# Sums made ahead for the first feed-forward's first group alone, their loads behind VectorE, a ring of five raw tiles, and the memory stage's pools in another order

## The chip, the cores and the metric

The kernel runs on one core of one Trainium2 chip. The metric is device time in microseconds (us) of one execution, as the median of the runs; lower is better. Everything is float32 in DRAM.

## The reference, cut to what matters

One layer of a streaming encoder block works on 256 tokens of width 2048, with 256 memory tokens:

```python
x = x + 0.5 * swiglu(rms_norm(x, ffn1_norm), ffn1_w_up, ffn1_w_down)   # ffn1, hidden width 5632
h = rms_norm(x, mix_norm); proj = h @ w_in                             # the middle: two recurrences, gates
x = x + (sigmoid(gate_A) * y_A @ w_a + sigmoid(gate_B) * y_B @ w_b) @ w_out
x = x + cross_attention(rms_norm(x, xattn_norm), rms_norm(mem, mem_norm), wq, wkv, wo)
x = x + 0.5 * swiglu(rms_norm(x, ffn2_norm), ffn2_w_up, ffn2_w_down)   # ffn2, the same shape as ffn1
return rms_norm(x, final_norm)
def swiglu(h, w_up, w_down):
    gate, up = split(h @ w_up, 2); return (silu(gate) * up) @ w_down
```

Nearly all of the arithmetic is the product of the activations with weights that are each read once. The change touches how ffn1's and ffn2's up weights are prepared.

## The kernel before, in words

**Two parts per weight.** A weight tile is 128 x 2048 float32, 1 MiB, a "piece". TensorE multiplies a rounded format, so each piece is cut into a high part h, which ScalarE rounds (`split`, L147), and a low part l = raw - h, which VectorE subtracts (L148). Three products (h with the high activations `xh`, h with their low part `xl`, l with `xh`) stand for one exact one.

**Stages.** The memory stage computes values and keys of the memory tokens (32 pieces of `wvm` and `wk`; it ends at about 185 us). ffn1 follows to about 868 us, then the middle to about 1798 us, then ffn2. A feed-forward has 11 groups of hidden columns. A group has 8 up pieces, numbered 0 to 7, and from the second group on it is followed by some pieces of the down projection (`ffn_order`: two after groups 1 and 2, four later).

**Seven products for eight.** The up projection is done on 512-column blocks by a scheme that needs seven block products where eight would be usual, and needs sums of blocks. The sums of a piece are three VectorE instructions (L335, L337, L339) which write the tile `td`; `td` is then cut into a high and a low part (`tl`) like a weight. A string (`FIRST`, L46) gives each up piece of ffn1 a letter, in the order in which the pieces are used:

- `f`: load, three sums, l by VectorE.
- `a` ("added"): load, three sums, but l of the raw blocks without VectorE: ScalarE writes -h (L344), and a DMA issued by GpSimd reads the weight a second time and adds it on top (L345, 768 KB). ScalarE makes h after it (L346).
- `r` ("ready"): the sums have been made earlier and stored to DRAM as a tile `t`. Then the piece needs two loads: three of its blocks (768 KB, L318) and `td<-t` (1 MiB, L323), and no sum.

**Sums made ahead.** `make_ahead` (L205 to L215) makes one `t`: GpSimd issues the load of a `prep` tile (L208), VectorE makes four subtractions (L213), GpSimd issues the store (L214). `beside` (L219) starts one every few pieces: for ffn1's `r` pieces during the memory stage, for ffn2's during the middle. `with tc.issue_after(ins)` puts what follows behind `ins` only on the engine on which `ins` runs, so around L208 (GpSimd) with a VectorE instruction it orders nothing.

**Who waits for whom.** `weights` prepares pieces two ahead. Loads are issued by SP in one row, each when its tile is free; SP stands still while the next one is not. Raw tiles come from `rawp` (3 tiles) and, in ffn1, one more (`raw1`, every fourth, L272). `h` and `l` have 3 tiles each. In ffn1 `td` and `tl` come from a ring `wide` of 4, and a ready piece's `td` does too. In the memory stage other pools stand at the same addresses: `scope` gives pools memory in the order in which they are named, so the order decides which tile of ffn1 must wait for which tile of the memory stage. `mem` (6 tiles) holds operands of the memory products, which TensorE reads until the stage's last product; `prep`, `tmp`, `tmp2` and `norms` come free earlier. `three` (L600 to L606) issues a piece's products: L604 those with h, L606 those with l and `tl`. `ev` (L690 to L702) marks a group's end.

Of the kernel before, what the change touches and what calls it, by code (L numbers as in the profile page):

```python
# [8 lines left out]
F32 = mybir.dt.float32  # L9
# [4 lines left out]
P = 128  # L14
# [5 lines left out]
NG = DFF // 512  # L20
# [22 lines left out]


PIECES = "f1 a3 f0 a4 f2 a5 a6 f7"
FIRST = ["r1 r3 f0 a4 f2 a5 a6 f7"] + [PIECES.replace("f2", "r2") if g in (1, 2, 3) else PIECES for g in range(1, NG)]  # L46


def first(g):
# [23 lines left out]

def adds(name, e):

    return name == "ffn1" and e[0] == "fast" and f"a{e[2]}" in FIRST[e[1]]


def sums_ready(name, e):
# [8 lines left out]
def block_kernel(ctx: ExitStack, tc: tile.TileContext, xT, xin, memT, vec, gfin, bgate, lruw, wu1, wd1, win, wv,  # L88
                 wg, wab, wout, wq, wk, wvm, wo, wu2, wd2, out_):
    nc = tc.nc  # L90
    pe, dve, act, sp = nc.tensor, nc.vector, nc.scalar, nc.sync
# [65 lines left out]
    def plan_ffn(name, wu, wd):  # L157
        for e in orders[name]:
            src = wd[e[4], e[3]] if e[0] == "down" else wu[e[1], e[2]]
            kind = "fast" if e[0] == "fast" else "plain"  # L160
            if e[0] == "down" and 0 < e[4] < NG - 1 and e[4] % 2 == 0 and e[3] % 2:
                kind = "added"
            if adds(name, e):
                kind = "fast added"
            if kind == "fast" and (e[1] < 4 if name == "ffn2" else False):
                kind = "fast early"
            if sums_ready(name, e):
                kind = "ready"
                t = kept.tile([P, 2048], F32, name=f"t{e[1]}_{e[2]}")
                (made_first if name == "ffn1" else made_ahead).append((src, t))  # L170
                src = src, t
            plan.append(((name,) + e, src, kind))
# [29 lines left out]

    head, rest = [], {}

    def make_ahead(src, to):  # L205

        t = scoped["prep"].tile([P, 2048], F32, name="prep", tag="prep")
        nc.gpsimd.dma_start(t, src)  # L208
        yield
        b = [t[:, i * 512:(i + 1) * 512] for i in range(4)]  # L210
        with tc.issue_after(done["low"]):
            for o, x, y in ((1, 0, 1), (0, 0, 2), (2, 2, 1), (3, 3, 2)):
                dve.tensor_tensor(out=b[o], in0=b[x], in1=b[y], op=ALU.subtract)  # L213
        nc.gpsimd.dma_start(to, t)  # L214
        yield  # L215
# [3 lines left out]
    def beside(i):  # L219

        if under_way and (i >= under_way[0][0] or "prep" not in scoped):
            next(under_way.pop(0)[1])
        if "prep" not in scoped or i < turn[0]:
            return
        if i < first_ffn:
            if made_first:
                turn[0] = i + 5 if len(made_first) > 1 else first_middle + 2
                steps = make_ahead(*made_first.pop(0))
                with tc.issue_after(done["low"]):
                    next(steps)  # L230
                under_way.append((i + 3, steps))
        elif made_ahead and i < first_second - 4:
            early = "scores" in scoped
            turn[0] = i + (2 + len(made_ahead) % 2 if early else 3 if len(made_ahead) % 3 else 2)
            steps = make_ahead(*made_ahead.pop(0))
            next(steps)
            under_way.append((i + (2 if early or "kt" in scoped else 3), steps))
# [34 lines left out]
    def raw_tile():  # L272

        if "raw2" in scoped and next(loads) % 5 > 2:
            return scoped["raw2"].tile([P, 2048], F32, name="raw2", tag="raw2")
        if "raw1" in scoped and next(loads) % 4 == 3:
            return scoped["raw1"].tile([P, 2048], F32, name="raw1", tag="raw1")
        return rawp.tile([P, 2048], F32, name="raw", tag="raw")

# [9 lines left out]
    def prepare(src, kind, opens=None):  # L289

        if kind == "added":
            raw, l = begun.pop(0)
            h = hp.tile([P, 2048], F32R, name="h", tag="h")
            done["high"] = act.activation(h, raw, ACT.Copy).ins
            return h, l
        first = opens == 0
        raw = begun.pop(0) if first else raw_tile()
        n = 2048 if opens is None else 512
        if kind == "plain":
            h, l = split_tiles()  # L300
            for a in range(0, 2048, n):
                if a or not first:
                    sp.dma_start(raw[:, a:a + n], src if opens is None else in_blocks(src, n)[a // n * P:][:P])
                if first and a == n:
                    sp.dma_start(opening[1], block(528, 512))
                if first and not a:
                    dve.tensor_scalar(out=h[:, :n], in0=raw[:, :n], scalar1=1.0, scalar2=None, op0=ALU.mult)
                if opens is not None:
                    mem_operand(4 * opens + a // n)
                if first and not a:  # L310
                    done["low"] = dve.tensor_tensor(out=l[:, :n], in0=raw[:, :n], in1=h[:, :n].bitcast(F32),
                                                    op=ALU.subtract).ins
                else:
                    split(h[:, a:a + n], l[:, a:a + n], raw[:, a:a + n])
            return h, l
        if kind == "ready":
            src, t = src
            sp.dma_start(raw[:, 512:], src[:, 512:])  # L318
            if "raw2" not in scoped and "wide" in scoped:
                td = scoped["wide"].tile([P, 2048], F32, name="td", tag="wide")  # L320
            else:
                td = raw_tile()
            sp.dma_start(td, t)  # L323
        else:
            sp.dma_start(raw, src)
            early = kind == "fast early"
            if early:
                td = slot(name="td")
            elif "raw2" in scoped:
                td = raw_tile()  # L330
            else:
                td = scoped["wide"].tile([P, 2048], F32, name="td", tag="wide")
            third, fourth = (raw[:, :512], raw[:, 512:1024]) if early else (td[:, 1024:1536], td[:, 1536:])
            two = [v[:, a:a + 1024].rearrange("p (i n) -> p i n", i=2) for v, a in ((td, 0), (raw, 512))]
            dve.tensor_tensor(out=two[0], in0=raw[:, None, :512].broadcast_to([P, 2, 512]), in1=two[1],  # L335
                              op=ALU.subtract)
            dve.tensor_tensor(out=third, in0=raw[:, 1024:1536], in1=td[:, :512], op=ALU.subtract)  # L337
            if not early:
                dve.tensor_tensor(out=fourth, in0=raw[:, 1536:], in1=third, op=ALU.subtract)  # L339
        h, l = split_tiles()  # L340
        if kind != "fast added":
            split(h[:, 512:], l[:, 512:], raw[:, 512:])
        else:
            act.activation(l[:, 512:], raw[:, 512:], ACT.Copy, scale=-1.0)  # L344
            nc.gpsimd.dma_start(l[:, 512:], src[:, 512:], accum_op=ALU.add)  # L345
            done["high"] = act.activation(h[:, 512:], raw[:, 512:], ACT.Copy).ins  # L346
        halves = [td[:, a:a + 1024] for a in ((0,) if kind == "fast early" else (0, 1024))]
        if kind == "fast early":
            dve.tensor_tensor(out=fourth, in0=raw[:, 1536:], in1=third, op=ALU.subtract)
            halves.append(raw[:, :1024])  # L350
        th = hp.tile([P, 2048], F32R, name="h", tag="h")
        if "wide" in scoped:
            tl = scoped["wide"].tile([P, 2048], F32R, name="tl", tag="wide")
        else:
            tl = lp.tile([P, 2048], F32R, name="tl", tag="l")
        for a, t in zip((0, 1024), halves):
            split(th[:, a:a + 1024], tl[:, a:a + 1024], t)
        return (h, l), (th, tl)
# [123 lines left out]
            return r  # L482


    FFN1_POOLS = dict(wide=4, hd=1, raw1=1)
    FFN2_POOLS = dict(wide=2, raw2=2, hid=1, hd=1)

    class TokenSquares:
# [377 lines left out]
            split(s[:, :512], s[:, 512:], f)  # L866
            nc.gpsimd.dma_start(kept_v[2 * g + t], s)

    with scope(mem=6, tmp=6, tmp2=1, norms=1, prep=1):
        for g in range(4):  # L870
            values.append((g, [bank(), bank()]))
            for kq in range(4):
                rows_product(values[-1][1], ms.tiles, weights("mv", g, kq), 4 * kq, kq == 0, kq == 3, g == kq == 0)
            if g:
                keep_values()
        ks = Operands()
        for m in range(KT):
            ks.add(summed(product(ms.tiles, weights("k", m))[0]))
            if not m:
                keep_values()  # L880
            if m % 2:
                nc.gpsimd.dma_start(kept_k[m // 2], ks.cur)
# [590 lines left out]
```

## Time and profile before

| | |
|---|---|
| time, median of 3 runs (lowest to highest) | 2472.39 us (2471.56 to 2485.05) |
| the profiled execution | 2474.72 us, its span 2473.0 us |
| mean granted TensorE clock | 0.992 |
| busy: PE / VectorE (DVE) / ScalarE (ACT) / GpSimd (POOL) | 2408.2 / 2100.1 / 1510.1 / 131.7 us |
| DMA moved | 711.07 MB, 288 GB/s in the mean |

The span is the time from the first to the last instruction of the profiled execution; the 1.7 us beside it lie outside. A group row reads: line, engine, operation, output<-input by the program's names, shape, count, then busy time and mean ns, then the idle time before. A timeline row reads: start, duration, the same names, count, and in brackets the engine's idle time before and what ended it. A windows row reads: the stretch, its length, then busy time and count of PE, PEld, DVE, ACT and POOL, the granted TensorE clock, the DMA engines' share and GB/s. SPq and POOLq are issues of DMA.

### The profile page before, as it was taken

The numbers are of one execution on the slowest core, as the hardware profiler recorded it, in microseconds if no ns is written. First come the engines' busy times: TensorE is split into PE (matmuls) and PEld (weight loads), VectorE is DVE, ScalarE is ACT, GpSimd is POOL, SyncE is SP. The second block draws the span as 40 slices with busy tenths as digits, with TensorE's granted clock in tenths as the row PEclk, the third lists the DMA queues.
The fourth block names the chain that finished last, engine by engine and source line by source line (L and its number), as shares of the span: only waits on it lengthen the run. The fifth ranks groups of instructions, "written<-read, shape, count | busy, mean of one in ns | idle before, by whom it ended". The sixth has DMA issues, their size and how long they took to land.

```text
span 2473.0 us, 30918 instructions
## 1 busy us (share of the span) xinstructions
PE 2408.2 (97%) x12044; PEld 1997.1 (81%) x12044; DVE 2100.1 (85%) x2359; ACT 1510.1 (61%) x1551; POOL 131.7 (5%) x213
## 2 busy tenths in 40 slices
PE   9997888999999999999999999999999999999998
PEld 7885666888888888888888888888887788888887
DVE  7777888999999967778788877777799998999895
ACT  6655666777777754445457434554676666666663
POOL 0100000000000000000000000010000000000000
PEclk9998999999999999999999999999999999999999
DMA  8997778889999958887988998898687778787773
GB/s 314 351 343 239 221 228 244 271 272 276 275 277 276 276 196 332 303 317 286 347 310 285 384 342 335 313 358 305 255 322 264 279 273 288 271 290 274 285 274 150
DMA packets 109106, 711.07 MB, mean 288 GB/s; under 512 B 12128, under 2 KB 12640, under 8 KB 36256
## 3 DMA queue, kind: packets, MB, share of 16 engines
q1 hardware_dynamic: 78912, 519.56, 56.3%
q0 software_dynamic: 29904, 189.28, 25.7%
q8 instruction: 94, 1.54, 0.2%
q14 instruction: 52, 0.43, 0.0%
q10 hardware_dynamic: 144, 0.26, 0.0%
HBM read 637.62 MB, written 71.43 MB: 287 GB/s over the span
## 4 chain that ended last, share of the span: by engine, by line
PE 74%; DVE 4%; issue 3%; DMA 3%; ACT 2%; POOL 0%; ACTq 0%; POOLq 0%; DVEq 0%
PE acc L604 26%; PE acc L606 13%; PE acc L368 8%; PE acc L393 7%; PE acc L394 6%; PE acc L399 6%; PE acc L371 4%; DMA raw<-wu 2%; ACT h L147 1%; DVE l L148 1%; DMA l<-wu 1%; DVE tl L148 1%; PE acc L644 1%; PE acc L540 1%; PE acc L994 0%
## 5 line engine op out<-in xcount | busy, mean ns | idle before, releaser
L147 ACT ACTIVATE h<-raw 128x2048 fp32r<-128x2048 f32 (+3 forms) x558 | 834.9, 1522 | 602.7 <-PE acc L394 178.8
L148 DVE TENSOR_TENSOR l<-raw,h 128x2048 fp32r<-128x2048 f32 (+2 forms) x392 | 801.7, 2048 | 191.9 <-ACT h L147 189.0
L604 PE MATMUL acc<-h,xh 128*128 128x512 f32 x1230 | 483.2, 396 | 18.3 <-ACT h L147 17.5
L604 PE MATMUL acc<-h,xl 128*128 128x512 f32 x1230 | 479.4, 392 | 0.0
L604 PE MATMUL acc<-h,hidop 128*128 128x512 f32 x1408 | 354.9, 391 | 0.0
L604 PEld LDWEIGHTS acc<-h,hidop 128*128 128x128 f32 x1408 | 262.5, 188 | 54.3 <-ACT h L147 0.7
L604 PEld LDWEIGHTS acc<-h,xh 128*128 128x128 f32 x1230 | 232.9, 189 | 81.6 <-ACT h L147 32.3
L393 PE MATMUL acc<-h,ops 128*128 128x512 f32 x704 | 276.3, 392 | 0.0
L394 PE MATMUL acc<-h,ops 128*128 128x512 f32 x704 | 274.3, 390 | 0.0
L604 PEld LDWEIGHTS acc<-h,xl 128*128 128x128 f32 x1230 | 232.8, 189 | 47.2
L148 DVE TENSOR_TENSOR tl<-td,h 128x1024 fp32r<-128x1024 f32 x182 | 221.2, 1220 | 43.7 <-ACT h L147 43.0
L147 ACT ACTIVATE h<-td 128x1024 fp32r<-128x1024 f32 x182 | 189.8, 1054 | 105.9 <-DVE td L335 33.6
L368 PE MATMUL acc<-ops,h 128*128 128x512 f32 x896 | 219.2, 395 | 0.0
L148 DVE TENSOR_TENSOR tl<-raw,h 128x1024 fp32r<-128x1024 f32 x166 | 196.5, 1219 | 11.7 <-ACT h L147 10.0
L606 PE MATMUL acc<-tl,xh 128*128 128x512 f32 x696 | 204.0, 394 | 0.6 <-DVE tl L148 0.6
L368 PEld LDWEIGHTS acc<-ops,h 128*128 128x128 f32 x896 | 165.3, 189 | 33.0
L606 PE MATMUL acc<-l,hidop 128*128 128x512 f32 x704 | 189.5, 389 | 0.0
L606 PE MATMUL acc<-l,xh 128*128 128x512 f32 x534 | 155.7, 399 | 29.8 <-DMA l<-wu 23.3
L399 PE MATMUL acc<-l,ops 128*128 128x512 f32 x704 | 174.0, 389 | 0.0
L213 DVE TENSOR_TENSOR prep<-prep 128x512 f32<-128x512 f32 x232 | 159.4, 687 | 5.8 <-DMA prep<-wu 2.3
L606 PEld LDWEIGHTS acc<-tl,xh 128*128 128x128 f32 x696 | 130.9, 190 | 30.9 <-DVE tl L148 4.2
L606 PEld LDWEIGHTS acc<-l,hidop 128*128 128x128 f32 x704 | 132.1, 188 | 27.7
(268 smaller groups left out, 2853.9 us busy)
## 6 DMA issues: line engine op xcount, KB each, us to landing
raw<-wu SPq DMA_DIRECT2D x118, 1024.0 KB, 6.5
raw<-wd SPq DMA_DIRECT2D x88, 1024.0 KB, 7.0
prep<-wu POOLq DMA_DIRECT2D x58, 1024.0 KB, 7.0
t<-prep POOLq DMA_DIRECT2D x58, 1024.0 KB, 5.8
raw<-t SPq DMA_DIRECT2D x54, 1024.0 KB, 5.7
raw<-wu SPq DMA_DIRECT2D x58, 768.0 KB, 5.9
raw<-win SPq DMA_DIRECT2D x40, 1024.0 KB, 6.7
l<-wu POOLq DMA_DIRECT2D x43, 768.0 KB, 9.6
```

The source lines that it names most:

```text
L147: done["high"] = act.activation(h, raw, ACT.Copy).ins
L148: done["low"] = dve.tensor_tensor(out=l, in0=raw, in1=h.bitcast(F32), op=ALU.subtract).ins
L213: dve.tensor_tensor(out=b[o], in0=b[x], in1=b[y], op=ALU.subtract)
L368: pe.matmul(acc, h[:, k * P:(k + 1) * P], xs[k], start=k == 0, stop=False)
L371: done["product"] = pe.matmul(acc[:, :T], l[:, k * P:(k + 1) * P], xs[k][:, :T], start=False, stop=k == KT - 1).ins
L393: pe.matmul(accs[t], x[:, t * P:][:, :P], h[j], start=first and j == 0, stop=False)
L394: pe.matmul(accs[t], x[:, T + t * P:][:, :P], h[j], start=False, stop=False)
L399: done["product"] = pe.matmul(accs[t], x[:, t * P:][:, :P], l[j], start=False, stop=last and j == 3).ins
L540: pe.transpose(acc[:, z * T + t * P:][:, :P], tile[:, t * 512 + (2 * y + z) * P:][:, :P], ident)
L604: pe.matmul(acc, a, b, start=start, stop=False)
L606: pe.matmul(acc, ah, bl, start=False, stop=stop)
L644: pe.transpose(acc[:, z * T + t * P:][:, :P], hid[t][:, (2 * y + z) * P:][:, :P], ident)
```

## The change

1. `FIRST`: group 0 goes from "r1 r3 f0 a4 f2 a5 a6 f7" to "r1 r3 r0 a4 r2 a5 a6 f7"; in groups 1, 2 and 3 piece 2 goes from `r` to `f`. Made ahead for ffn1 are 4 pieces where there were 5.
2. `adds`: in ffn2's groups 1, 2 and 3 piece 5 gets its low part as an `a` piece does.
3. `make_ahead(behind=True)` for ffn1's pieces: VectorE writes one column of `prep` behind the latest l, so the load of `prep` waits for VectorE.
4. The cadence of ffn2's sums in the middle: pieces between two starts go from 2 and 3 in turn to 3, 3, 2 in the first part, and the other way round later.
5. The raw ring in ffn1: two of five tiles from `raw1` (2 tiles), and `wide` has 3; a ready piece's `td` is a raw tile.
6. The memory stage's pools are named in the order prep, tmp, tmp2, norms, mem (before: mem, tmp, tmp2, norms, prep).

```diff
-FIRST = ["r1 r3 f0 a4 f2 a5 a6 f7"] + [PIECES.replace("f2", "r2") if g in (1, 2, 3) else PIECES for g in range(1, NG)]
+FIRST = ["r1 r3 r0 a4 r2 a5 a6 f7"] + [PIECES] * (NG - 1)
...
-    return name == "ffn1" and e[0] == "fast" and f"a{e[2]}" in FIRST[e[1]]
+    if name == "ffn2":
+        return e[0] == "fast" and 0 < e[1] < 4 and e[2] == 5
+    return e[0] == "fast" and f"a{e[2]}" in FIRST[e[1]]
...
-    def make_ahead(src, to):
+    def make_ahead(src, to, behind=False):
 
         t = scoped["prep"].tile([P, 2048], F32, name="prep", tag="prep")
+        if behind:
+            with tc.issue_after(done["low"]):
+                dve.memset(t[:, :1], 0.0)
         nc.gpsimd.dma_start(t, src)
...
-                steps = make_ahead(*made_first.pop(0))
-                with tc.issue_after(done["low"]):
-                    next(steps)
+                steps = make_ahead(*made_first.pop(0), behind=True)
+                next(steps)
...
-            turn[0] = i + (2 + len(made_ahead) % 2 if early else 3 if len(made_ahead) % 3 else 2)
+            turn[0] = i + 2 + (len(made_ahead) % 3 > 0 if early else len(made_ahead) % 2)
...
-        if "raw1" in scoped and next(loads) % 4 == 3:
+        if "raw1" in scoped and next(loads) % 5 > 2:
...
-            if "raw2" not in scoped and "wide" in scoped:
-                td = scoped["wide"].tile([P, 2048], F32, name="td", tag="wide")
-            else:
-                td = raw_tile()
+            td = raw_tile()
             sp.dma_start(td, t)
...
-    FFN1_POOLS = dict(wide=4, hd=1, raw1=1)
+    FFN1_POOLS = dict(wide=3, hd=1, raw1=2)
...
-    with scope(mem=6, tmp=6, tmp2=1, norms=1, prep=1):
+    with scope(prep=1, tmp=6, tmp2=1, norms=1, mem=6):
```

**Where instructions move, 1: GpSimd's queue at the start.** Before, its first load has nothing to wait for.

```order
L1465 UNCONDITIONAL_BRANCH [waits barrier_Pool_Activation_PE_DVE_SP_gather]
L208 DMA prep<-wu 128x2048
L860 DMA rmem<-rstd 128x256 [waits DVE_49]
L867 DMA v_164<-vs 128x1024 [waits DVE_49]
L867 DMA v_165<-vs 128x1024 [waits DVE_49]
```

After, in the same place of the row:

```order
L1466 UNCONDITIONAL_BRANCH [waits barrier_Pool_Activation_PE_DVE_SP_gather]
L213 DMA prep<-wu 128x2048 [waits DVE_49]
L861 DMA rmem<-rstd 128x256 [waits DVE_49]
L868 DMA v_163<-vs 128x1024 [waits DVE_49]
L868 DMA v_164<-vs 128x1024 [waits DVE_49]
```

Nothing changes its place; the first load gets a wait for VectorE, whose row has the one-column write behind the l of a full-size weight piece, some eight pieces in.

**2: SP's queue at the end of the memory stage**, from the load of piece 3's three blocks on (`t0_3` is the stored sum of group 0's piece 3, `t0_0` and `t0_2` those of pieces 0 and 2; `wu1` is a weight). Before:

```order
L318 DMA raw_1821<-wu1 128x1536
L325 DMA raw_1863<-wu1 128x2048
L325 DMA raw1_1938<-wu1 128x2048
L325 DMA raw_1900<-wu1 128x2048
L325 DMA raw_1975<-wu1 128x2048
L323 DMA td_1823<-t0_3_96 128x2048
L325 DMA raw_2013<-wu1 128x2048
```

After:

```order
L323 DMA raw_1817<-wu1 128x1536
L325 DMA raw_1819<-t0_3_96 128x2048
L323 DMA raw_1859<-wu1 128x1536
L325 DMA raw1_1861<-t0_0_97 128x2048
L327 DMA raw1_1894<-wu1 128x2048
L323 DMA raw_1932<-wu1 128x1536
L325 DMA raw_1934<-t0_2_98 128x2048
```

The sum of piece 3 is loaded right behind the piece and into a raw tile; before, it stood behind four other loads. The sums of pieces 0 and 2 are two loads more, each with a shorter load of the piece itself. `raw1_1861` and `raw1_1894` lie where `mem` lay.

**3: VectorE in ffn1's group 1**, around pieces 4 and 2. Before (`td_2243` is piece 4's sums, `raw1_2279` and `td_2281` belong to piece 2, `td_2316` to piece 5):

```order
L339 TENSOR_TENSOR td_2243<-raw_2241,td_2243 128x512
L148 TENSOR_TENSOR l_2284<-raw1_2279,h_2283 128x1536
L148 TENSOR_TENSOR tl_2253<-td_2243,h_2252 128x1024
L148 TENSOR_TENSOR tl_2288<-td_2281,h_2287 128x1024 x2
L335 TENSOR_TENSOR td_2316<-raw_2314 128x1024
```

After (`td_2235` is piece 4's sums, `td_2273` piece 2's, `td_2310` piece 5's):

```order
L340 TENSOR_TENSOR td_2235<-raw1_2233,td_2235 128x512
L336 TENSOR_TENSOR td_2273<-raw1_2271 128x1024
L150 TENSOR_TENSOR l_2278<-raw1_2271,h_2277 128x1536
L150 TENSOR_TENSOR tl_2245<-td_2235,h_2244 128x1024
L338 TENSOR_TENSOR td_2273<-raw1_2271,td_2273 128x512
L150 TENSOR_TENSOR tl_2282<-td_2273,h_2281 128x1024
L340 TENSOR_TENSOR td_2273<-raw1_2271,td_2273 128x512
L336 TENSOR_TENSOR td_2310<-raw_2308 128x1024
```

Three instructions of sums for piece 2 come in, between the low parts of pieces 4 and 2. Groups 2 and 3 change alike.

More of the change, by code (lines that the diff above doesn't have):

```diff
@@ L162, in plan_ffn @@
                 kind = "added"
+            if kind == "fast" and name == "ffn2" and e[1] < 4:
+                kind = "fast early"
             if adds(name, e):
-                kind = "fast added"
-            if kind == "fast" and (e[1] < 4 if name == "ffn2" else False):
-                kind = "fast early"
+                kind += " added"
             if sums_ready(name, e):
@@ L315, in prepare @@
             return h, l
+        early = "early" in kind
         if kind == "ready":
@@ L325, in prepare @@
             sp.dma_start(raw, src)
-            early = kind == "fast early"
             if early:
@@ L340, in prepare @@
         h, l = split_tiles()
-        if kind != "fast added":
+        if "added" not in kind:
             split(h[:, 512:], l[:, 512:], raw[:, 512:])
@@ L346, in prepare @@
             done["high"] = act.activation(h[:, 512:], raw[:, 512:], ACT.Copy).ins
-        halves = [td[:, a:a + 1024] for a in ((0,) if kind == "fast early" else (0, 1024))]
-        if kind == "fast early":
+        halves = [td[:, a:a + 1024] for a in ((0,) if early else (0, 1024))]
+        if early:
             dve.tensor_tensor(out=fourth, in0=raw[:, 1536:], in1=third, op=ALU.subtract)
```

## The prediction

> **What bounds the kernel now.** The page comes first: which engine is full, and over the whole span.
>
> ```profile
> span 2473.0 us, 30918 instructions
> PE 2408.2 (97%) x12044; PEld 1997.1 (81%) x12044; DVE 2100.1 (85%) x2359; ACT 1510.1 (61%) x1551; POOL 131.7 (5%) x213
> ```
>
> TensorE (PE) is idle for 2473.0 - 2408.2 = 64.8 us in all, and part of its busy time is at a lower clock. A gain has to come out of these two, so the second view is the windows, one stretch for each group of ffn1 (from one group's `ev` to the next), two stretches of the middle, and three of ffn2's groups.
>
> ```profile
> 185.00:242.40 57.40, 44.12 (x174) 34.70 (x172) 42.30 (x42) 32.92 (x30) 4.04 (x5) 0.88 0.78 239
> 242.40:291.80 49.40, 39.34 (x163) 30.39 (x164) 42.54 (x49) 33.18 (x33) 2.59 (x3) 0.93 0.75 227
> 291.80:355.40 63.60, 54.15 (x225) 42.66 (x224) 55.49 (x59) 39.83 (x35) 3.47 (x4) 0.95 0.74 227
> 355.40:418.00 62.60, 53.25 (x225) 42.01 (x225) 55.02 (x59) 39.80 (x36) 3.46 (x4) 0.95 0.75 231
> ...
> 606.00:667.20 61.20, 61.20 (x274) 49.99 (x272) 59.95 (x63) 45.31 (x39) 4.37 (x5) 1.00 0.92 275
> 1862.00:1912.30 50.30, 49.69 (x219) 39.62 (x217) 48.32 (x48) 30.60 (x31) 0.00 (x0) 1.00 0.75 276
> 1912.30:1965.80 53.50, 51.32 (x225) 41.01 (x224) 52.20 (x51) 33.83 (x32) 0.00 (x0) 1.00 0.72 272
> 1965.80:2029.40 63.60, 62.82 (x281) 51.53 (x279) 60.67 (x58) 42.25 (x38) 0.89 (x1) 1.00 0.75 264
> 868.00:1302.00 434.00, 430.50 (x3029) 368.48 (x3029) 337.96 (x447) 216.25 (x249) 27.26 (x51) 1.00 0.80 298
> 1302.00:1798.00 496.00, 496.00 (x2391) 416.35 (x2390) 387.51 (x483) 270.77 (x334) 38.34 (x72) 1.00 0.86 323
> ```
>
> Read downwards: in the late group (606 to 667) PE is full, and VectorE (DVE) is busy for 59.95 of 61.20 us, so it idles 1.25 us. One product there costs 61.20 / 274 = 0.2234 us. The middle is full but for 3.5 us. In the first four groups PE is idle for 13.28, 10.06, 9.45 and 9.35 us, and the granted clock is below 1. That is where this kernel can still gain. Third, the view of waits and the timeline say for what PE waits.
>
> ```profile
> 9.37 0.50 PE L393 MATMUL acc<-h,ms 128*128 128x512 f32 x1 [2.76 <-ACT h L147]
> ```
> ```profile
> PE acc L606 <- DMA l<-wu: 21.9, 5, 5.8
> PE acc L604 <- ACT h L147: 11.7, 7, 8.7
> PE acc L606 <- DVE l L148: 6.5, 6, 1.4
> ```
> ```profile
> 200.87 0.80 PE L604 MATMUL acc<-h,xh 128*128 128x512 f32 x1 [8.72 <-ACT h L147]
> ...
> 333.67 1.65 PE L606 MATMUL acc<-l,xh 128*128 128x512 f32 x3 [5.85 <-DMA l<-wu]
> ```
>
> The first is a stall in the opening; the three rows of waits are those of 185 to 420 us; the last two are the worst of them. 8.72 us is a wait for the high part of piece 3's stored sum in group 0, and each of groups 1 to 3 has one wait of about 5.8 us for a low part that a DMA accumulates (piece 4).
>
> **Part A, the opening.** The first load of `prep` now waits for VectorE, some eight pieces later.
>
> ```profile
> 1.28 0.69 POOL L208 DMA_DIRECT2D prep<-wu  x1 [0.83 <-POOLq L1460]
> ...
> 8.69 0.63 ACT L147 ACTIVATE h<-raw 128x512 fp32r<-128x512 f32 x1 [3.57 <-DMA raw<-wvm]
> ```
> ```profile
> 2.00:8.60 6.60, 4.15 (x18) 3.16 (x16) 1.82 (x4) 1.88 (x5) 0.00 (x0) 1.00 1.00 364
> ```
>
> The DMA engines are full from 2.0 to 8.6 us at 364 GB/s, and the `prep` load is 1.049 MB of that: 1.049 MB / 364 GB/s = 2.9 us earlier for the quarters of the weight that ScalarE waits for (8.69). PE's stall of 2.76 us goes. The bounds are 0 (another of the many loads in the same stretch is then the last) and 2.9. I take 2.7, near the row of the stall itself. The one-column write on VectorE is at most some 0.1 us, before data that nobody waits for. Moved, the load lies beside later weights; the opening's is the only stall of PE over 1 us that the trace has before 185 us. The Trainium skill, "DMA: Bandwidth & Descriptors" (Anatomy of one DMA), fits a DMA as a fixed 2.0 us and bytes over 436 GB/s; by that the load moves for an estimated 2.4 us and this part would be 0.3 us less; the row of 364 GB/s decides for me.
>
> **Part B, into group 0.** Before, piece 3's stored sum is a tile of `wide` at addresses of the memory operands, behind four other loads in SP's row.
>
> ```profile
> 199.76 2.00 ACT L147 ACTIVATE h<-td 128x1024 fp32r<-128x1024 f32 x2 [11.80 <-DMA td<-t]
> ```
> ```profile
> 177.50 10.03 SPq L325 DMA_DIRECT2D raw<-wu  x4
> 187.58 0.44 SPq L323 DMA_DIRECT2D td<-t  x1
> ```
> ```profile
> 200.87:206.10 5.23, 5.23 (x12) 4.17 (x13) 5.23 (x5) 5.23 (x5) 0.92 (x1) 0.50 0.00 0
> ```
>
> After, it takes the place of the first of those four, at 177.5, and lands some 12 us later (187.58 to 199.7 before) at the latest: 189.5. PE needs it at 200.87 - 8.72 = 192.15. So the 8.72 us and the half clock behind it (5.23 us at 0.50, 2.6 lost) go. What comes next? The sums of pieces 0 and 2 are loads now: VectorE is rid of two times 1.22 + 0.69 + 0.69 = 2.6 us (rows in part C), 42.30 - 5.2 = 37.1 us, and PE's own work is 174 x 0.2234 = 38.9 us. Neither DVE nor PE explains more than 38.9. But piece 4's low part still comes by an accumulating DMA, and its load (`raw1`, where `mem` lay) still waits for the memory stage's last products, at 185.0. By 10 us to landing (the row of `td<-t` in part C) it is there at 195.0; ScalarE writes -h in 1.47 us (same place), GpSimd issues a good us later, at 197.5, and 9.1 us (the late groups' median, there too) make 206.6. PE gets there after 3 pieces of 21 products and the first 14 of piece 4: 185.0 + 77 x 0.2234 = 202.2. A stall of 4.4 us is left, and with it a half clock like the one in the row, 2.6: group 0 takes 38.9 + 4.4 + 2.6 = 45.9 where it took 57.4. **Gain 11.5.** Bounds: 18.5 (no stall), and 4 if that part lands 7.5 us later still, as it could behind the loads of the next pieces.
>
> On the clock, the Trainium skill, "TensorE: Matmul & The Clock Gate" (Part 1), has the array at half clock after an idle window of about 3.4 us and back after about 3.4 us of work. By that the stall left over costs 1.7 and not 2.6, and the gain would be 0.9 us more. The trace has 5.23 us here, so it does not hold the 3.4 at this place.
>
> **Part C, groups 1 to 3.** Piece 2 is summed on VectorE again, in place of a second load.
>
> ```profile
> L335 DVE TENSOR_TENSOR td<-raw 128x1024 f32<-128x1024 f32 x8 | 9.7, 1217 | 0.0
> ...
> L148 DVE TENSOR_TENSOR l<-raw,h 128x1536 fp32r<-128x1536 f32 x4 | 7.0, 1750 | 0.0
> L339 DVE TENSOR_TENSOR td<-raw,td 128x512 f32<-128x512 f32 x8 | 5.5, 686 | 0.1
> L337 DVE TENSOR_TENSOR td<-raw,td 128x512 f32<-128x512 f32 x8 | 5.5, 684 | 0.0
> ```
> ```profile
> L148 DVE TENSOR_TENSOR tl<-td,h 128x1024 fp32r<-128x1024 f32 x16 | 19.4, 1220 | 7.8 <-ACT h L147 7.8
> ```
> ```profile
> l<-wu POOLq DMA_DIRECT2D x11, 768.0 KB, 10.9
> ...
> td<-t SPq DMA_DIRECT2D x3, 1024.0 KB, 10.0
> ```
> ```profile
> l<-wu POOLq DMA_DIRECT2D x20, 768.0 KB, 9.1
> ```
> ```profile
> L344 ACT ACTIVATE l<-raw 128x1536 fp32r<-128x1536 f32 x4 | 5.9, 1471 | 0.0
> ```
>
> These are, in this order: VectorE's groups from 606 to 667 us; its costliest in group 2 (291.8 to 355.4); DMA issues from 242 to 418 us with the median from issue to landing, and from 544 to 851; ScalarE's copy for -h, 606 to 667.
>
> DVE gets 2.59 us more in each (1.217 + 0.686 + 0.684, group of 606 to 667): 45.1, 58.1 and 57.6 us. That is more than PE's own work (163 and 225 products: 36.4 and 50.3 us), so DVE sets these groups, and its idle time is the question. In group 2 it idles 7.8 us, all for ScalarE's high part, which comes late because PE, which frees its tiles, stands for the accumulated part. The stored sum's load shares the DMA engines with that part: from 242 to 418 us it takes 10.9 us in the median, from 544 to 851 us, without such loads, 9.1. So the wait shrinks from 5.8 to about 4.0, and 2.6 of it DVE now works on piece 2's sums, which wait for nobody. DVE idles 1.25 as in the late group and 1.4 more: the groups take 47.8, 60.8 and 60.3. **Gain 1.6 + 2.8 + 2.3 = 6.7.** Bounds: idle as in the late group, 11.0; or DVE's present idle kept whole and the sums on top, -7.8. From group 4 on nothing changes but `wide`: 0 here, a rival below.
>
> **Part D, ffn2's piece 5.** In groups 1 to 3 VectorE loses a subtraction of 1.75 us (third row of part C), ScalarE gets a copy of 1.47 and GpSimd an accumulating DMA of 768 KB.
>
> ```profile
> 1933.66 0.50 PE L604 MATMUL acc<-h,xh 128*128 128x512 f32 x1 [1.63 <-ACT h L147]
> ```
>
> PE idles there 0.61 + 2.18 + 0.78 = 3.6 us, the longest for ScalarE behind VectorE's sums. I take **1.5**; at best 3.6; at worst each accumulated part is as late as in ffn1's group 2.
>
> **Part E, the cadence in the middle.** As many sums in all but one (57 for 58), PE full before and after: **0**, within 3 either way, since DMA has 14 to 20% to spare in the two stretches.
>
> **Sum.** 2.7 + 11.5 + 6.7 + 1.5 = 22.4 us off the span of 2473.0: 2450.6. The profiled execution took 2474.72, so 1.7 us lie around the span, and 2452.3 follows for it. It was 2.3 above the median of 2472.39; off the median I get and forecast **2450**.
>
> **The rivals.**
> *DVE takes part C back*: the wait for the accumulated part stays at 5.8 and the sums come on top (C = -7.8). For it: DVE is the fuller engine there. Against: in the row above the idle is one wait, beside which the sums can run. 2472.4 - 2.7 - 11.5 - 1.5 + 7.8 = 2464.5.
> *The transition stays*: the stored sum of piece 0, whose tile lies where `mem` lay, takes the place of piece 3's as the late load, so that part B brings nothing: 2472.4 - 10.9 = 2461.5. Against: PE needs it 21 products, 4.7 us, later than piece 3's, and it is the second and not the fifth load to wait.
> *ffn2's accumulated parts come late* in all three groups, 5.8 and 2.6 us each: 25.2 lost for the 1.5: 2450.0 + 1.5 + 25.2 = 2477. Against: the DMA share is 0.72 to 0.75 there, and at 0.92 (606 to 667) four such parts in each group cost PE nothing.
> *Slower: the ring of three.* With `wide` at 3, the sums of a piece wait for PE's last product with `tl` two pieces back. In the late groups:
>
> ```profile
> 754.77 1.07 PE L606 MATMUL acc<-tl,xh 128*128 128x512 f32 x4
> ...
> 755.90 1.22 DVE L335 TENSOR_TENSOR td<-raw 128x1024 f32<-128x1024 f32 x1
> ```
>
> They start 0.06 us behind that product's end already now, so the new wait bites only by its own latency x. Six pieces of a group with it, less the 1.25 us that DVE has to spare, in groups 4 to 10: 7 x (6x - 1.25). It makes the kernel slower by over 12.4 only from x = 1.04 us on (34.8 us against the 22.4); at 1.1 the time is 2472.4 - 22.4 + 37.5 = 2487.5. Against: waits of PE and DVE on each other end within 0.1 us in the rows here.
>
> **How the numbers follow.** About 0.5%, 12.4 us, is what a measurement of this kernel can tell from no change: faster is below 2460.0, slower above 2484.8. Chances: the forecast 0.70, DVE takes C back 0.11, the transition stays 0.08, ffn2 late 0.06, the ring of three 0.05. The forecast's own bounds are 2437 (B 18.5, C 11.0, D 2.5, A 2.9 make 34.9) and about 2461; the second and third case reach to 2465, and a small gain of either lies below 2460, which I count as 0.08 for faster: 0.78. Same is 0.17, slower 0.05. The range is 2437 to 2465.
>
> **What would show it right or wrong.** Right: no PE stall before 15 us; no 8.7 us stall at 200 but one of 3 to 6 for `l<-wu` soon after; group 0 at 44 to 48 us; groups 1 to 3 at 47 to 49 and 60 to 62 with DVE over 95% busy; groups 4 to 10 at 61.2. Wrong: the late groups longer than 61.2 with DVE waiting for PE's L606; a stall for `l<-wu` in ffn2; the first groups unchanged.

## The result and the profile after

The changed kernel takes 2486.84 us in the median (2482.76 to 2496.02) where the kernel before, run beside it on the same chips, takes 2476.85 (2471.56 to 2485.05), 18 runs each. The ratio is 1.0043 with a 95% interval of 1.0033 to 1.0052: slower, by some 10 us, where 22 us less were forecast (from the 2472.4 us of the first three runs). The profiled execution has a span of 2482.3 us, 9.3 above that of before.

The page's first part, and the windows of the same stages as before (group 0 from 185 us to its `ev`, groups 1 to 3, a late group, then ffn2's groups 1 to 4):

```profile
span 2482.3 us, 31013 instructions
PE 2414.1 (97%) x12044; PEld 2000.4 (81%) x12044; DVE 2097.9 (85%) x2359; ACT 1513.9 (61%) x1552; POOL 133.2 (5%) x214
```
```profile
185.00:229.60 44.60, 39.49 (x167) 31.95 (x166) 36.70 (x37) 32.52 (x28) 3.19 (x4) 0.96 0.98 346
229.60:285.40 55.80, 43.41 (x165) 31.69 (x164) 44.09 (x51) 33.35 (x32) 3.45 (x4) 0.91 0.67 189
285.40:349.80 64.40, 55.70 (x224) 42.44 (x224) 57.55 (x62) 40.04 (x37) 3.48 (x4) 0.95 0.72 212
349.80:412.80 63.00, 54.23 (x224) 41.35 (x224) 57.48 (x62) 39.97 (x35) 3.48 (x4) 0.97 0.73 217
...
599.20:660.40 61.20, 61.20 (x273) 50.01 (x272) 59.79 (x63) 45.53 (x40) 4.32 (x5) 1.00 0.91 274
1804.70:1858.80 54.10, 50.47 (x221) 41.25 (x220) 46.09 (x42) 36.82 (x35) 0.89 (x1) 0.97 0.82 294
1858.80:1917.50 58.70, 52.81 (x229) 43.20 (x228) 51.03 (x50) 35.06 (x33) 0.87 (x1) 0.94 0.72 262
1917.50:1978.80 61.30, 53.28 (x225) 43.20 (x224) 51.33 (x50) 35.17 (x33) 0.88 (x1) 0.92 0.69 253
1978.80:2038.90 60.10, 59.76 (x268) 49.18 (x267) 55.50 (x54) 37.97 (x35) 0.86 (x1) 1.00 0.75 261
```

Set against the same rows of before, this is a balance by place:

| stage | before | after | difference |
|---|---|---|---|
| up to the end of group 0 | 242.4 | 229.6 | -12.8 |
| ffn1 groups 1, 2, 3 | 49.4, 63.6, 62.6 | 55.8, 64.4, 63.0 | +7.6 |
| ffn2 groups 1, 2, 3 | 49.5, 50.3, 53.5 | 54.1, 58.7, 61.3 | +20.8 |
| ffn2 group 4 | 63.6 | 60.1 | -3.5 |
| all other stages together | | | -2.8 |
| span | 2473.0 | 2482.3 | +9.3 |

Up to the end of group 0 it gained nearly what was forecast. Groups 1 to 3 of ffn1 gave more than half of it back, and ffn2's groups 1 to 3 cost 20.8 us, more than the whole gain. The waits of PE from 1800 to 2040 us, after and before:

```profile
PE acc L607 <- DMA l<-wu: 17.1, 3, 7.5
```
```profile
PE acc L604 <- ACT h L147: 3.6, 6, 1.6
```

Three waits for the accumulated low part, 17.1 us in all, have come where there was none. The timeline shows one of them: ScalarE writes -h as soon as the raw tile has landed, GpSimd issues, and PE comes for the part 6 us later (1905.24 - 5.89 = 1899.35), while the DMA needs 11.7.

```profile
1891.63 1.49 ACT L345 ACTIVATE l<-raw 128x1536 fp32r<-128x1536 f32 x1 [0.46 <-DMA raw<-wu]
```
```profile
1893.56 0.87 POOL L346 DMA_DIRECT2D l<-wu  x1 [56.54 <-ACT l L345]
```
```profile
1905.24 1.22 PE L607 MATMUL acc<-l,xh 128*128 128x512 f32 x2 [5.89 <-DMA l<-wu]
```

In ffn1's group 2 the same kind of wait is still there, and VectorE stands for 6 us behind it. The timeline has PE's wait for piece 4's low part, PE's last products with piece 4's `tl`, and VectorE's next sums, piece 5's; the fourth row is VectorE's group from 285.4 to 349.8 us, its last figures the idle time and who ended it:

```profile
326.33 1.65 PE L607 MATMUL acc<-l,xh 128*128 128x512 f32 x3 [4.60 <-DMA l<-wu]
...
334.02 0.62 PE L607 MATMUL acc<-tl,xh 128*128 128x512 f32 x2
```
```profile
334.68 1.23 DVE L336 TENSOR_TENSOR td<-raw 128x1024 f32<-128x1024 f32 x1 [5.99 <-PE acc L607]
```
```profile
L336 DVE TENSOR_TENSOR td<-raw 128x1024 f32<-128x1024 f32 x8 | 9.8, 1220 | 6.0 <-PE acc L607 6.0
```

### The profile page after: what moved, and what is told of

It is laid out like the page before. It is cut to its first block, busy times and chain, and to the rows that moved or that the text cites. A ratio compares the mean times of both kernels' runs of the same rounds, so it can differ in the third digit from the quotient of the medians.

```text
span 2482.3 us, 31013 instructions
## 1 busy us (share of the span) xinstructions
PE 2414.1 (97%) x12044; PEld 2000.4 (81%) x12044; DVE 2097.9 (85%) x2359; ACT 1513.9 (61%) x1552; POOL 133.2 (5%) x214
## 3 DMA queue, kind: packets, MB, share of 16 engines
q8 instruction: 94, 1.54, 0.2%
## 5 line engine op out<-in xcount | busy, mean ns | idle before, releaser
L605 PEld LDWEIGHTS acc<-h,hidop 128*128 128x128 f32 x1408 | 262.3, 188 | 55.8 <-ACT h L149 1.5
L149 ACT ACTIVATE h<-td 128x1024 fp32r<-128x1024 f32 x176 | 184.4, 1055 | 108.2 <-PE acc L605 48.2
L150 DVE TENSOR_TENSOR tl<-td,h 128x1024 fp32r<-128x1024 f32 x176 | 213.8, 1219 | 23.4 <-ACT h L149 22.5
L150 DVE TENSOR_TENSOR tl<-raw,h 128x1024 fp32r<-128x1024 f32 x172 | 203.4, 1219 | 14.5 <-ACT h L149 13.7
L607 PEld LDWEIGHTS acc<-l,xh 128*128 128x128 f32 x534 | 101.6, 193 | 74.3 <-DMA l<-wu 43.1
```

Source lines behind the costliest of these rows:

```text
L150: done["low"] = dve.tensor_tensor(out=l, in0=raw, in1=h.bitcast(F32), op=ALU.subtract).ins
L605: pe.matmul(acc, a, b, start=start, stop=False)
L607: pe.matmul(acc, ah, bl, start=False, stop=stop)
```

## The experiments

Thirteen kernels were run. Ratios are to the kernel before on the same chip.

**e1: ffn2's accumulated parts taken out of the changed kernel.**

```diff
-        return e[0] == "fast" and 0 < e[1] < 4 and e[2] == 5
+        return False
```

> The changed kernel with part 2 undone alone: ffn2's piece 5 in groups 1 to 3 gets its low part from VectorE again. Theory: the three accumulated parts land 11.6 to 12.0 us after their issue and cost PE 3.6, 5.9 and 7.5 us of stall and the half clock behind them; without them ffn2's groups 1 to 3 go back from 54.1, 58.7 and 61.3 to about 49.5, 50.3 and 53.5 us, group 4 from 60.1 to 63.6, and the kernel is about 17 us faster than the changed one, near 2470, some 6 to 8 under the kernel before. Rival: the time is lost in ffn2 for another reason that came with the change (what the middle leaves behind, another order of the stored sums); then the groups stay within 2 us of the changed kernel's and the time within 3 us.

Measured: 2465.71 us, ratio 0.9951 (0.9932 to 0.9970). ffn2's groups 1 to 4:

```profile
1811.00:1860.40 49.40, 49.40 (x223) 40.84 (x222) 47.16 (x43) 35.30 (x33) 0.00 (x0) 1.00 0.83 310
1860.40:1909.70 49.30, 49.06 (x219) 39.78 (x217) 48.43 (x48) 30.93 (x31) 0.00 (x0) 1.00 0.73 278
1909.70:1961.70 52.00, 50.37 (x225) 41.26 (x224) 52.00 (x51) 34.10 (x32) 0.00 (x0) 1.00 0.74 284
1961.70:2023.60 61.90, 61.41 (x274) 50.42 (x273) 59.07 (x57) 40.44 (x36) 0.89 (x1) 1.00 0.75 266
```

The first three are back at 49 to 52 us, and the clock at 1.00. The four groups take 212.6 us where the changed kernel takes 234.2. The theory holds, and without this part the change is faster than the kernel before.

**e4: the same part alone, put into the kernel before** (the lines of `adds` and the kind strings from the diff).

> The kernel before with part 2 of the change alone: piece 5 of ffn2's groups 1 to 3 by ScalarE and an accumulating DMA. Theory: the same loss as in the changed kernel, three PE stalls of 3.6 to 7.5 us for the accumulated part in ffn2 and about 17 us more than the kernel before; ffn1 untouched. Rival: the parts are late only because of how the changed kernel reaches ffn2; then the loss here is under 5 us.

Measured: 2498.54 us, ratio 1.0085 (1.0062 to 1.0109), 21 us slower. PE's waits in ffn2:

```profile
PE acc L609 <- DMA l<-wu: 16.8, 3, 7.9
```

Put in alone it costs 21 us (0.0085 of 2480), and taken out it gives 0.0092 back, 23 us: that this part makes the kernel slower is shown.

**e2: the rings as before (four raw tiles, `wide` of 4) in the changed kernel.** A ready piece's sum stays in a raw tile.

```diff
-    FFN1_POOLS = dict(wide=3, hd=1, raw1=2)
+    FFN1_POOLS = dict(wide=4, hd=1, raw1=1)
-        if "raw1" in scoped and next(loads) % 5 > 2:
+        if "raw1" in scoped and next(loads) % 4 == 3:
```

> The changed kernel with wide at 4 and one raw1 tile, every fourth load, as before; all else as changed. Theory: in ffn1's groups 1 to 3 VectorE stands 5.5 to 6.0 us because the sums of piece 5 want the tile of piece 4's tl, which PE releases only after its wait for the accumulated low part; with four tiles the sums of piece 5 (2.6 us) run in that wait, VectorE's idle before L336 falls under 1 us, and each of the three groups is about 2.6 us shorter, 6 to 9 in all. Rival: the ring of three is harmless; VectorE then waits as long for ScalarE's high part (as in the kernel before, 6.5 us a group), and the groups stay within 1 us of 55.8, 64.4 and 63.0.

Measured: 2487.80 us, ratio 1.0031 (1.0017 to 1.0045), the changed kernel's within the interval. The groups take 56.2, 64.2 and 62.9 us. VectorE in group 2:

```profile
L150 DVE TENSOR_TENSOR tl<-td,h 128x1024 fp32r<-128x1024 f32 x17 | 20.7, 1220 | 6.8 <-ACT h L149 6.8
L336 DVE TENSOR_TENSOR td<-raw 128x1024 f32<-128x1024 f32 x8 | 9.8, 1219 | 0.0
```

```profile
332.96 1.49 ACT L347 ACTIVATE h<-raw 128x1536 fp32r<-128x1536 f32 x1 [6.94 <-PE acc L605]
```

The idle time of 6.0 before L336 is gone, and 6.8 stand before `tl`: the wait has only changed its name. The theory of the ring falls, the rival holds: `tl` needs ScalarE's high part, and ScalarE has stood 6.94 us for a tile that PE gives back after its own wait (the row above).

**e3: piece 4 of groups 1 to 3 without the accumulating DMA** (`a4` to `f4`).

> The changed kernel with piece 4 of ffn1's groups 1 to 3 as f in place of a: its low part comes from VectorE (1.75 us more there), and no accumulating DMA is left in these groups but those of pieces 3, 5 and 6. Theory: the wait for piece 4's accumulated part (4.3 to 4.7 us and its half clock) sets these groups; without it they take VectorE's work of 46 to 59 us and 1 to 2 idle, about 49, 61 and 61 us where the changed kernel takes 55.8, 64.4 and 63.0: 10 to 14 us less in all. Rival: VectorE alone sets them, its idle only follows PE; then each becomes 1.75 us longer, 5 in all. Second rival: the next accumulated part (piece 5's) takes the place of piece 4's as the late one, and little changes.

Measured: 2490.11 us, ratio 1.0044 (1.0029 to 1.0059). The groups take 61.7, 65.1 and 65.2 us, longer by 5.9, 0.7 and 2.2. PE in 341 to 342 us:

```profile
341.39 1.22 PE L607 MATMUL acc<-l,xh 128*128 128x512 f32 x2 [5.21 <-DMA l<-wu]
```

This is piece 5's part, issued at 332.98 us: the second rival. Without piece 4's the next accumulated part is the late one.

**e5: piece 2 of group 1 ready again, without ffn2's parts** (five sums made ahead, as before).

> The changed kernel without ffn2's accumulated parts, and with piece 2 of ffn1's group 1 as a ready piece again (five sums made ahead, as many as before). Theory: VectorE's 2.6 us of sums are what a group that VectorE bounds pays, wherever it waits besides: group 1 goes from 55.8 to 52 to 53 us and the kernel is 2 to 4 us faster than the one without ffn2's accumulated parts; the wait for piece 4's part stays or grows. Rival: group 1 lost its 6 us because group 0 became faster and left less prepared ahead, not by the sums; then group 1 stays at 55 to 56.

Measured: 2472.16 us, ratio 0.9974 (0.9960 to 0.9989); e1 has 0.9951. Group 1 takes 57.9 us, not less than e1's 56.4, though VectorE has three sums less to make for it. So the sums on VectorE were not what group 1 paid for. And group 0 ends at 237.1 where e1's ends at 232.6.

**e6: ffn1's `a` pieces begun one piece earlier**, on top of e1. The load, -h and the accumulating DMA are issued ahead of the piece before, as the kernel does for the down pieces.

```diff
-            if plan and plan[0][2] == "added":
-                begun.append(begin_added(plan[0][1]))
+            if plan and "added" in plan[0][2]:
+                begun.append(begin_added(plan[0][1], 0 if plan[0][2] == "added" else 512))
```

> The changed kernel without ffn2's accumulated parts, and with ffn1's a pieces begun one piece earlier: load, -h by ScalarE and the accumulating DMA are issued before the piece ahead of it is prepared, as the down pieces' are. Theory: the parts are late because -h stands in ScalarE's row behind the halves of the piece before, which wait for VectorE; one piece (5 to 7 us) earlier covers the 4.3 to 4.7 us, PE's waits for l<-wu in groups 0 to 3 go, VectorE's idle there falls to 1 or 2 us a group, and the three groups take 47 to 49, 60 and 60 us: 8 to 14 us less than without it. Rival: the DMA takes longer where it is issued earlier, or ScalarE then stands for a free l tile with the next pieces' high parts behind it: the waits only change their name, and the time stays within 3 us or grows.

Measured: 2447.69 us, ratio 0.9872 (0.9857 to 0.9886). Groups 1 to 3:

```profile
236.40:280.60 44.20, 39.94 (x166) 29.50 (x167) 44.03 (x51) 32.23 (x32) 1.74 (x2) 1.00 0.73 219
280.60:337.90 57.30, 53.05 (x224) 39.80 (x223) 57.23 (x62) 40.14 (x35) 3.48 (x4) 1.00 0.79 238
337.90:396.40 58.50, 54.42 (x224) 41.28 (x224) 57.50 (x62) 40.07 (x36) 3.48 (x4) 0.97 0.77 234
```

VectorE is busy for 44.03 of 44.20 us, 57.23 of 57.30 and 57.50 of 58.50: now it bounds the first two of these groups and nearly the third, and they are 11.6, 7.1 and 4.5 us shorter than in the changed kernel. No wait for `l<-wu` is left. Against e1, which lacks the early begin alone, the kernel gains 0.0079, 20 us. The cause shows in piece 4's rows of group 2: -h by ScalarE, the issue by GpSimd, and PE's products with the part. The changed kernel first (PE comes at 321.73 us and waits until 326.33, as shown above), then e6:

```profile
314.67 1.47 ACT L345 ACTIVATE l<-raw 128x1536 fp32r<-128x1536 f32 x1
...
316.54 0.87 POOL L346 DMA_DIRECT2D l<-wu  x1 [17.13 <-ACT l L345]
```
```profile
293.83 1.49 ACT L289 ACTIVATE l<-raw 128x1536 fp32r<-128x1536 f32 x1 [2.09 <-PE acc L611]
...
295.72 0.87 POOL L290 DMA_DIRECT2D l<-wu  x1 [9.15 <-DMA l<-wu]
...
314.62 0.84 PE L611 MATMUL acc<-l,xh 128*128 128x512 f32 x3
```

From the issue to PE's need there are 18.9 us where there were 5.2. The DMA itself takes no less time: a median of 9.4 us from 236 to 396, and 7.2 in the changed kernel from 230 to 413. It starts earlier against PE's need.

**e7: as e6, with ffn2's parts as well, begun early.**

> As the run before, but with ffn2's accumulated parts of piece 5 in groups 1 to 3, begun one piece earlier as well. Theory: the DMA needs 11.6 to 12.0 us there and PE comes for it 3.6 to 7.5 us before; a piece earlier is 4.7 us of PE, so two of the three stalls go and one of 2 to 3 us is left: some 12 us less lost than with them late, still no gain against the run without them. Rival: what is saved on VectorE (1.75 us a group) then shows as a gain of 1 to 3 us against it.

Measured: 2453.61 us, ratio 0.9890 (0.9874 to 0.9906). PE waits for no accumulated part in ffn2 any more, better than expected, though the DMA's median is 11.6 us still. Yet the three groups take 50.2, 52.0 and 53.9 us, against 49.5, 49.8 and 52.0 in e6 without these parts. Part 2 of the change brings nothing even when its parts come in time. In groups 1 and 2 VectorE was not the bound (47.24 of 49.50 us and 48.57 of 49.80 in e6). In group 3 it was (52.00 of 52.00, as in e1's row), and there e7's VectorE has less to do but stands for 2.9 us, 2.8 of them for ScalarE's high parts:

```profile
1890.30:1944.20 53.90, 52.24 (x225) 40.57 (x224) 50.98 (x50) 35.08 (x34) 0.88 (x1) 1.00 0.79 287
```

**e8: the old pool order in the changed kernel.**

> The changed kernel with the memory stage's pools in the old order alone. Theory: the order decides whether group 0's first tiles wait for the memory stage's last product; with the old one wide lies on mem and raw1 on mem and prep, the third piece's tl or sums come late, and PE stalls 3 to 6 us more at the start of group 0. Rival: the gain in group 0 came from the ready pieces and the ring, whose first tiles are free early in either order; then group 0 changes by under 1.5 us.

Measured: 2487.30 us, ratio 1.0035 (1.0021 to 1.0049): no difference in the time. In the profile group 0 ends at 236.6 us, 7.0 later, its stall for the accumulated part at 6.7 where it was 4.3; but group 1 gives 2.7 of it back, and ffn1 ends at 848.3, 4.1 later. That is not enough to blame the order: e1 and e12, with the new order and the same preparation of group 0, have stalls of 6.7 and 6.4 us there and end group 0 at 232.6 and 234.9, while the changed kernel and e9 end it at 229.6 and 230.2. What the order is worth at that place is not shown.

**e9: no one-column write ahead of the first `prep` load** (`behind=False`), one run.

> One look: the changed kernel without the one-column write, so that the first load of prep waits for nothing. Theory: the 1.0 to 1.1 us stall of PE near 9 us grows back to 2.1 to 2.8 us, as in the kernel before; the price of part 3 is 1 to 2 us. Rival: the opening's stall comes from the memory operands' own loads; then it stays at about 1.1.

Measured: the stall near 9 us is 1.48 us, in between. By the profiles of other kernels, it is 1.45 (e10), 1.98 (e13), 2.08 (e4) and 2.76 (before) without the wait, and from none (e5, e6, e11) to 1.54 (e12) with it. The sign is as forecast; the size is about 1 us, and differs as much between profiles.

**e10: the kernel before with the `a` pieces begun early, and nothing of the change.**

> The kernel before with ffn1's a pieces begun one piece earlier, and nothing of the change. Theory: the late accumulated part, and not the number of sums on VectorE, held groups 1 to 3; here VectorE has 2.6 us less in each of them than in the changed kernel begun early, so they take about 45, 57 and 57 us, and the kernel is 12 to 18 us faster than the kernel before; group 0 keeps its stall of 8.7 us for the stored sum of piece 3, and most of the gap to the changed kernel begun early (12 us in group 0, less 3 x 2.6) is there. Rival: the ready pieces' second load and SP's row hold these groups, and they stay above 60 us in groups 2 and 3.

Measured: 2495.59 us, ratio 1.0076 (1.0056 to 1.0096): slower, against the theory; groups 2 and 3 stay above 60, as the rival had it, at 61.5 and 61.9 us, though better than before (group 1 takes 46.7). But the late groups now take 62 to 67, and there ScalarE waits for raw tiles:

```profile
543.80:610.80 67.00, 62.87 (x274) 51.38 (x273) 61.07 (x63) 45.46 (x39) 4.33 (x5) 0.97 0.84 252
```
```profile
L147 ACT ACTIVATE h<-raw 128x1536 fp32r<-128x1536 f32 x4 | 5.9, 1487 | 8.4 <-DMA raw<-wu 6.4 <-PE acc L608 2.0
```
```profile
580.39 1.48 ACT L285 ACTIVATE l<-raw 128x1536 fp32r<-128x1536 f32 x1 [3.23 <-DMA raw<-wu]
```
```profile
582.88 0.71 PE L608 MATMUL acc<-h,xh 128*128 128x512 f32 x1 [4.13 <-ACT h L147]
```

The load of the piece that is begun early comes late. ScalarE stands for it, with the high part that PE wants next behind it in its row. That the load is late for want of a free raw tile is what e13 goes on to test.

**e13: e10 with the change's rings** (five raw tiles, `wide` of 3, a ready piece's sum in a raw tile), nothing else of the change.

> The kernel before with ffn1's a pieces begun early (as e10) and the change's rings (five raw tiles, wide at 3, a ready piece's sum in a raw tile), nothing else of the change. Theory: with four raw tiles the load of a piece that is begun early is issued so late that ScalarE stands for it (3.2 us in group 6) with the high part of the piece before behind it; with five it is issued a tile earlier, groups 4 to 10 go from 62.5 to 67 us back to 61.2 or 61.4, groups 1 to 3 to 57 to 59 in the last two, and the kernel is 20 to 35 us faster than e10. Rival: the ready pieces of groups 1 to 3 or the old pool order make e10 slow; then groups 4 to 10 stay above 62.

Measured: 2445.04 us, ratio 0.9860 (0.9839 to 0.9880), some 50 us less than e10:

```profile
238.70:282.30 43.60, 39.66 (x165) 30.81 (x165) 42.95 (x49) 31.95 (x32) 1.71 (x2) 0.96 0.75 240
282.30:337.30 55.00, 51.26 (x223) 40.42 (x224) 53.83 (x57) 39.80 (x36) 3.47 (x4) 1.00 0.82 256
337.30:396.10 58.80, 52.13 (x225) 40.55 (x225) 56.20 (x60) 40.00 (x35) 3.45 (x4) 1.00 0.84 252
...
580.60:642.00 61.40, 61.27 (x273) 49.85 (x273) 60.15 (x63) 45.85 (x38) 4.37 (x5) 1.00 0.92 273
```

```profile
L147 ACT ACTIVATE h<-raw 128x1536 fp32r<-128x1536 f32 x4 | 6.0, 1488 | 1.7 <-PE acc L605 1.6
```

The late groups are back at 61.4 us, ScalarE's idle time before its high parts is 1.7 us (519 to 581) where e10 had 8.4, and group 2 is shorter than expected. So the rings, worth nothing in the changed kernel (e2), are what makes the early begin pay. Five raw tiles, `wide` of 3 and the stored sum in a raw tile were put in together; that the fifth raw tile is the one that counts fits ScalarE's wait, but was not tested alone. This kernel has the ready pieces in groups 1 to 3 and the old pool order, so neither made e10 slow. This version beats both kernels; it can't be told from e6, since their intervals overlap.

**e11: e6 with piece 2 of group 1 ready.**

> The run with ffn1's a pieces begun early and without ffn2's accumulated parts (e6), and piece 2 of group 1 ready again. Theory: with no late part VectorE bounds group 1, so its 2.6 us of sums there now show: 1.5 to 2.6 us less than e6, under what the measurement can tell, and group 1 at 41.5 to 43 us where it took 44.2. Rival: the second load and a fifth sum made ahead in the memory stage cost what they save.

Measured: 2452.53 us, ratio 0.9892 (0.9878 to 0.9907), not faster than e6. Group 1 takes 43.9 us for 44.2, but group 0 ends at 245.5 for 236.4: the rival. With e5 (237.1 for 232.6) it is the second case in which group 0 ended later with a fifth sum made ahead, by more than VectorE saves. Each is one profile, and group 0's end differs by some 5 us between kernels that prepare it alike (see e8), so the cause is not shown.

**e12: e6 with group 0's `a` pieces not begun early.**

> e6 with group 0's a pieces prepared as in the changed kernel, and early only from group 1 on. Theory: in group 0 the early begin costs more (loads that come first wait for the memory stage, group 0 ends 4 to 7 us later than in the changed kernel) than the 4 to 7 us stall it takes away; so group 0 ends near 230 to 233 and the kernel is 3 to 6 us faster than e6, near 0.985 of the kernel before. Rival: group 0's end differs between executions by as much (229.6 and 232.6 with the same first group); then no difference to e6.

Measured: 2452.04 us, ratio 0.9888 (0.9871 to 0.9906), not faster than e6. The stall for piece 4's part in group 0 is back, at 6.4 us, and group 0 ends at 234.9 where e6's ends at 236.4; the early begin in group 0 costs nothing in sum. The theory falls.

## Why the prediction was wrong, point by point

**Part A** (2.7): the stall went from 2.76 to 1.12, as part of a difference that e9 and the other profiles put near 1 us. The sign fits the mechanism; the term was too large.

**Part B** (11.5): right. Up to the end of group 0 the span is 12.8 us shorter, part A's 1.6 in it, where A and B together were to bring 14.2. The 8.72 us stall is gone, group 0 takes 44.6 us (45.9 forecast), and the stall worked out as 4.4 us for piece 4's accumulated part is there:

```profile
206.36 1.22 PE L607 MATMUL acc<-l,xh 128*128 128x512 f32 x2 [4.29 <-DMA l<-wu]
```

That the size fits so well is in part luck: the same stall was 3.8 us in e9 and 6.7 in e1. The half clock that goes with it is the one of 206.0 to 209.4 us (0.51), 1.7 us lost and not 2.6. The 5.23 us that the forecast took over from before were the second half of a longer stretch at 0.50, from 195.9 to 206.1 us, which had begun in the old stall.

**Part C** (6.7 gained; 7.6 lost): this step failed. PE's wait for the accumulated part did shrink, from 5.8 to 4.6 in group 2 (4.0 forecast), and VectorE did work on piece 2's sums beside it. But "DVE idles 1.25 as in the late group and 1.4 more" is wrong: the forecast took the sums out of an idle time that it set beside PE's wait. VectorE's idle time comes later. It works on through the wait until it has no tile left, and then stands until PE frees one, at 334.68, 8 us after the wait's end, since PE has the piece's products still to do and the first of them at half clock. So the idle falls only from 8.1 (63.6 - 55.49) to 6.9 us (64.4 - 57.55), where 2.65 were forecast, and the new sums are longer than that. e2 shows that the tile doesn't matter, e6 that the lateness does: without it VectorE's work alone is left, 57.2 us.

The forecast had this as a rival, at 2.6 us lost in each group, 7.8 in all. That 7.6 were lost in all is luck: groups 2 and 3 lost 0.8 and 0.4, between forecast and rival, and group 1 lost 6.4. By e5 group 1 didn't pay for its sums. A second accumulated part is late there: PE waits 4.25 us for it at 239 us, where it waited 1.56 before, and the clock is at 0.50 for 10.2 us of the group where it was for 6.8. Group 0 had become faster; that this caused the longer wait was only argued.

**Part D** (1.5 gained; 17.3 lost with group 4): this step failed by its sign, and it decides the result. The rival had it, at 25.2 us and a chance of 0.06, and a stall for `l<-wu` in ffn2 was among the forecast's own signs of being wrong. Its argument against, "four such parts in each group cost PE nothing" in the late groups of ffn1, was no evidence: there PE comes later for the part. Piece 4's in the late group of the kernel before, 606 to 667 us (GpSimd's issue, then PE's products, with no wait), and the page's row of these DMAs over the whole span:

```profile
635.23 0.86 POOL L345 DMA_DIRECT2D l<-wu  x1 [10.06 <-ACT l L344]
```
```profile
646.36 0.84 PE L606 MATMUL acc<-l,xh 128*128 128x512 f32 x3
```
```profile
l<-wu POOLq DMA_DIRECT2D x43, 768.0 KB, 9.6
```

That is 11.1 us of lead, for a DMA that took 9.1 there in the median. In the changed kernel's ffn2 the leads are 8.4, 5.8 and 4.1 us. What should have been compared was the time from the issue to PE's need with the time from issue to landing, 9.6 us in the median in that row of the page; in ffn2 the DMA then took 11.6 to 12.0. The gain had little room too: the three rows that the forecast read as ffn2's groups 1 to 3 are groups 2 to 4 (the `ev`s of group 1 to 4 are at 1862.0, 1912.3, 1965.8 and 2029.4 us). In group 1 PE had no idle time at all, so that of the three groups is 2.8 us and not 3.6:

```profile
1812.50:1862.00 49.50, 49.50 (x224) 40.85 (x222) 47.26 (x44) 35.42 (x34) 0.00 (x0) 1.00 0.81 297
```

**Part E** (0) and the ring of three (a chance of 0.05): the late groups take 61.2 us as before, and the middle 960.5 for 961.6. Right.

ffn2's late parts came as their rival said, and the rival of part C came in part, at once. The forecast priced each alone, against an otherwise intact sum, and had no case for both.

## What to carry to other kernels

A low part that a DMA accumulates trades VectorE time for lead: it pays only where the time from its issue to its use is longer than the DMA's own, so compare those two for each place and start the chain (load, copy, issue) that much ahead; it gains nothing where VectorE isn't the bound (ffn2's groups 1 and 2). Before work is counted into an engine's idle time, find where that idle time begins and which tile ends it: it need not lie beside the wait that causes it. And a bigger ring is worth what is begun early with it: the same rings were worth nothing in the changed kernel and some 50 us between e10 and e13.

## What the runs showed of the hardware

The granted clock falls in stretches of 3.4 us or two or three of them: 3.4, 6.8 and 10.2 us at 0.50 in the changed kernel, the longest with the longest stall (7.5 us, until 1964.75). It can begin before the stall ends.

```profile
206.00:209.40 3.40, 3.04 (x7) 2.46 (x8) 0.00 (x0) 1.44 (x2) 0.03 (x1) 0.51 1.03 422
260.60:267.40 6.80, 5.01 (x12) 4.00 (x13) 4.18 (x5) 1.32 (x2) 0.87 (x1) 0.50 1.03 290
...
1960.50:1970.70 10.20, 5.95 (x14) 4.69 (x15) 3.65 (x3) 1.48 (x1) 0.00 (x0) 0.50 0.98 366
```

That fits the Trainium skill, "TensorE: Matmul & The Clock Gate" (Part 1), which has the clock set by free-running windows of about 3.4 us. But a full window of idle isn't needed: in e10 a stall of 2.25 us was followed by one at 0.51, while one of 2.29 in e13 was not (383.0 to 386.4 at 1.00).

```profile
647.97 0.79 PE L608 MATMUL acc<-h,xh 128*128 128x512 f32 x1 [2.25 <-ACT h L147]
```
```profile
647.80:651.20 3.40, 3.23 (x8) 2.55 (x9) 3.25 (x4) 2.18 (x3) 0.43 (x1) 0.51 0.94 178
```

An accumulating DMA of 768 KB took 11.6 us in ffn2, and in ffn1's groups 1 to 3 it took 7.2 in the changed kernel and 9.4 in e6, all in the median. The Trainium skill, "DMA: Bandwidth & Descriptors" (Anatomy of one DMA), has a fixed 2.0 us and bytes over 436 GB/s, an estimate of 3.8 us; the traces have about two to three times that beside the other loads. No run here had the engines to itself, so how much of it is the sharing and how much the accumulating stays open.
